# The RWKV recurrence in 45 named pieces: another order, 64x64 score products, and an inverse by two blocks of 8 and a corner

## The chip, the cores and the metric

The kernel runs on one core of one Trainium2 chip. The metric is device time in microseconds from launch to the last output. Before the change the median of three runs is 3890.82 us (3889.8 to 3914.53). TensorE is called PE below, VectorE DVE, ScalarE ACT, GpSimd POOL; SP is the engine that issues the DMAs.

## The reference, cut to what matters

Two blocks run one after the other on 512 tokens of width 1024. The first has a Fourier layer and an RWKV layer, each followed by a mixture of experts; the second has two attention layers with feed-forward parts. The change touches the recurrence of the RWKV layer alone. Per direction (forward and reversed) and per head (16 heads of 64) the reference scans the tokens one by one, first 256 context tokens, then the 512 tokens of x, with a 64x64 state:

```python
def step(s, inp):
    r_t, w_t, k_t, v_t, a_t, b_t = inp
    sa = jnp.einsum('bhvk,bhk->bhv', s, a_t)
    s = s * w_t[:, :, None, :] + sa[..., None] * b_t[:, :, None, :] + v_t[..., None] * k_t[:, :, None, :]
    return s, jnp.einsum('bhvk,bhk->bhv', s, r_t)
```

The outputs of the context tokens are not needed; only the state that they leave is.

## The kernel before, in words

`c_scan` (from L1357) does not go token by token but chunk by chunk: 64 tokens are one chunk, and a step of the loop takes one chunk of each of the two directions for all 16 heads. There are 12 steps: 4 of context, then 8 of x. Inside a chunk the recurrence is a triangular system of 64 unknowns per head. A step is done in three stages, which the loop of L1604 onwards overlaps: round `i` runs `products(i+2)` and `inverse(i+2)`, `merge(i+1)` and `advance(i)`; two rounds, -2 and -1, fill the pipeline.

- `products` (L1411): the scores of a chunk, 64x128 weights (`bk`) by 64 columns in context steps and 128 in x steps (`ar`), into `Aps` in PSUM (L1430); DVE multiplies them with a triangular mask into `GA` (L1434); PE turns `bk` (`bkp`, L1439) and ACT copies the result to `bkN` (L1441). This is done four times a step (two directions, two groups of four head pairs), each piece with two `Aps` tiles.
- `inverse` (L1447): the 16x16 diagonal blocks of the triangular matrices are brought onto lanes (ACT `Dg` L1453, DVE transpose `W` L1456, `A` L1458), and all of them are inverted by forward substitution: for the rows t = 1 to 15 one DVE product of t x t elements per lane (`pr`, L1464) and one DVE sum (L1465), each waiting for the one ahead.
- `merge` (L1468): two doublings, 16 to 32 to 64, by small products (`m` L1485, `tt` L1492, `m` L1506, `x` L1519; called m2, tt, m4 and x4 below) with DVE transposes (`T` L1479, `TT` L1480, `T` L1497) and ACT copies between them. After m4 the matrices in `GA` are overwritten by four DMAs (L1511) with what the state product needs; this is called the refill below.
- `advance` (L1526): the recurrence of the state: product `G` (L1542), copy `Gs`, product `U` with the inverse (L1551), copy `UV`, product `S` (L1568), then `sn` (DVE L1574), the decayed state `sd` (POOL L1562), and the new state `SV` (L1576), one half of the partitions by DVE and one by POOL. In x steps the output follows: `Yps` (L1584 and L1588) and its copy or sum into `Y` (L1597, L1599).

The order of the work is written as a string (L1603) of letters, one for a piece, in which G, U, S, Y stand for the pieces of `advance`, p, i and m or M for the next piece of the other stages:

```python
order = "M G p g p M pp M p mpp" + " U u pppp pp M pp m" + " p S pp i p M s m ii iii iii" + " Y i ii M i y ii m ii i"
```

This is not the order of the instructions on an engine. A planner takes the written order as a priority: it plays the program through with its own costs, and for each engine it takes, of the instructions that are ready by these costs, the one that was written first. What comes out is fixed; on the chip each engine then works its list strictly in turn. PSUM has eight banks: three for the scores (pool `pA`), two for the turns and the doublings (`pm`), three for G, U, S and the output (`pc`).

Of the kernel before, what the change touches and what calls it, by code (L numbers as in the profile page):

```python
# [11 lines left out]
F32 = mybir.dt.float32  # L12
# [24 lines left out]


# [1318 lines left out]
def c_scan(e, sp, PL, Y):  # L1357
# [4 lines left out]
    with ExitStack() as ctx:  # L1362
# [48 lines left out]
        def products(i):  # L1411


            st = sts[i]
            isc, chs = steps[i]
            na = 1 if isc else 2
            ga = st["GA"] = p3.tile([P, 2, ND, 2, 2, 64], F32, name="GA")
            bkN = st["bkN"] = p3.tile([P, 2, ND, P], F32, name="bkN")
# [4 lines left out]
            for d in range(2):  # L1423
                ar, bk = st["ar"][d], st["bk"][d]
                flat = lambda dt: bk[:, dt].rearrange("p a t -> p (a t)")
                for g in range(2):
                    pss = [pA.tile([P, 4, P], F32, name="Aps") for hh in range(2)]
                    for b in range(4):
                        for hh in range(2):
                            nc.tensor.matmul(pss[hh][:, b, :64 * na], flat(4 * g + b)[hv[hh]], ar[hv[hh], 4 * g + b, 0:na, :],  # L1430
                                             start=True, stop=True, tile_position=(64 * hh, 0))
                    yield
                    for hh in range(2):
                        tt_(ga[:, d, 4 * g:4 * g + 4, hh, 0:na, :].rearrange("p a r t -> p a (r t)"), pss[hh][:, :, :64 * na],  # L1434
                            bc(mgl[d][hh][:, :64 * na], 4), ALU.mult)
                    yield
                    ps = pm.tile([P, 4, P], F32, name="bkp", tag="mm")
                    for b in range(4):
                        nc.tensor.transpose(ps[:, b, :], flat(4 * g + b), e.ident)  # L1439
                    yield  # L1440
                    nc.scalar.copy(bkN[:, d, 4 * g:4 * g + 4, :], ps)  # L1441
                    yield

        def parts(st):
            return [q4(st["GA"], q)[:, :, :, q // 2, 0, :].rearrange("p c d t -> p (c d) t") for q in range(4)]

        def inverse(i):  # L1447

            st = sts[i]
            Ev = parts(st)  # L1450
            Dg = p1.tile([P, 16, 32], F32, name="Dg", tag="t3")
            for q in range(4):
                nc.scalar.copy(q4(Dg, q), Ev[q][:, :, bs(q % 2)])  # L1453
            yield
            W = p1.tile([P, 16, 32], F32, name="W", tag="t1")
            nc.vector.transpose(W, Dg.rearrange("p u (s t) -> p t s u", s=2))  # L1456
            A16 = p1.tile([P, 16, 16], F32, name="A16")
            nc.vector.scalar_tensor_tensor(A16, W[:, :, 0:16], h16[:, 0:1], W[:, :, 16:32], op0=ALU.mult, op1=ALU.add)  # L1458
            X = st["X"] = p1.tile([P, 16, 16], F32, name="X", bufs=2)
            nc.gpsimd.tensor_copy(X, e.tc_("eye16").rearrange("p (a b) -> p a b", a=16))  # L1460
            yield
            for t in range(1, 16):
                pr = p1.tile([P, 15, 15], F32, name="pr")
                tt_(pr[:, :t, :t], bc(A16[:, t, :t], t), X[:, :t, :t].rearrange("p i j -> p j i"), ALU.mult)  # L1464
                nc.vector.tensor_reduce(X[:, t, :t], pr[:, :t, :t], op=ALU.add, axis=AX.X)  # L1465
                yield

        def merge(i):  # L1468

            st = sts[i]  # L1470
            chs = steps[i][1]
            ga, X, Ev = st["GA"], st["X"], parts(st)
            Tx = p1.tile([P, 16, 2, 16], F32, name="Tx", tag="t2")
            for s in range(2):
                nc.scalar.activation(Tx[:, :, s, :], X, AF.Copy, scale=h16[:, s:s + 1])
            yield
            TT16 = p1.tile([P, 16, 32], F32, name="TT16")
            T16 = p1.tile([P, 16, 32], F32, name="T16")
            nc.vector.transpose(T16.rearrange("p u (s j) -> p j s u", s=2), Tx.rearrange("p t s j -> p j s t"))  # L1479
            nc.vector.transpose(TT16.rearrange("p u (s t) -> p t s u", s=2), Tx.rearrange("p t s j -> p t (s j)"))  # L1480
            yield
            ps = pm.tile([P, 16, 32], F32, name="m2", tag="mm")
            for u in range(16):
                for q in range(4):
                    nc.tensor.matmul(q4(ps, q)[:, u, :], Ev[q][:, u, bs(q % 2)], q4(T16, q)[:, u, :], start=True, stop=True, tile_position=pos(q, q))  # L1485
            yield
            nc.scalar.activation(M2[:, :, 0:16], ps[:, :, 0:16], AF.Copy, scale=h16[:, 1:2])
            yield
            ps = pm.tile([P, 16, 32], F32, name="tt2", tag="mm")
            for u in range(16):  # L1490
                for q in range(4):
                    nc.tensor.matmul(q4(ps, q)[:, u, :], q4(M2, q)[:, u, :], q4(TT16, q)[:, u, :], start=True, stop=True, tile_position=pos(q, q))  # L1492
            yield
            TT32 = p1.tile([P, 16, 32], F32, name="TT32")
            tt_(TT32, ps, TT16, ALU.add)
            T32 = p1.tile([P, 16, 32], F32, name="T32", tag="t2")
            nc.vector.transpose(T32, TT32)  # L1497
            TT64 = st["TT64"] = TT64s[i % 2]
            for h2 in (0, 2):
                nc.scalar.copy(q4(TT64, h2)[:, :, bs(0)], q4(TT32, h2))  # L1500
                nc.gpsimd.tensor_copy(q4(TT64, h2 + 1)[:, :, bs(1)], q4(TT32, h2 + 1))
            yield
            ps = pm.tile([P, 16, 32], F32, name="m4", tag="mm")
            for u in range(16):
                for h2 in (0, 2):
                    nc.tensor.matmul(q4(ps, h2 + 1)[:, u, :], Ev[h2][:, u, bs(1)], q4(T32, h2)[:, u, :], start=True, stop=True,  # L1506
                                     tile_position=pos(h2, h2 + 1))
            yield
# [3 lines left out]
            M4 = p1.tile([P, 16, 32], F32, name="M4", tag="t3")  # L1512
            for h2 in (0, 2):
                nc.scalar.copy(q4(M4, h2 + 1), q4(ps, h2 + 1))
            yield
            ps = pm.tile([P, 16, 32], F32, name="x4", tag="mm")
            for u in range(16):
                for h2 in (0, 2):
                    nc.tensor.matmul(q4(ps, h2)[:, u, :], q4(M4, h2 + 1)[:, u, :], q4(TT32, h2 + 1)[:, u, :], start=True, stop=True,  # L1519
                                     tile_position=pos(h2 + 1, h2))  # L1520
            yield
            for h2 in (0, 2):
                nc.scalar.copy(q4(TT64, h2)[:, :, bs(1)], q4(ps, h2))
            yield

        def advance(i):  # L1526

            isc, chs = steps[i]
            st = sts[i]
            ga, bkN, TT64, SV = (st[k] for k in ("GA", "bkN", "TT64", "SV"))  # L1530
            last = i == n - 1
            pl_ = [PL[d][:, chs[d], :] for d in range(2)]
            both = [(dt, hh) for dt in range(ND) for hh in range(2)]
            UV = [p3.tile([P, ND, 2, 64], F32, name="UV", bufs=2) for d in range(2)]
            for d in range(2):
                values(UV[d], chs[d])
            if not last:
                states(i + 1)
            ps = [pc.tile([P, ND, 64], F32, name="G", tag="c") for d in range(2)]
            for d in range(2):  # L1540
                for dt, hh in both:
                    nc.tensor.matmul(ps[d][hv[hh], dt, :], ga[:, d, dt, hh, 0, :], SV[d][:, dt, hh, :], start=True, stop=True, tile_position=(0, 64 * hh))  # L1542
            yield
            Gs = [p2.tile([P, ND, 64], F32, name="Gs") for d in range(2)]
            for d in range(2):
                nc.scalar.copy(Gs[d], ps[d])
# [803 lines left out]
```

## Time and profile before

| | |
|---|---|
| median of three runs | 3890.82 us |
| the profiled execution: its time | 3894.26 us |
| its span (first to last instruction) | 3892.5 us |
| PE busy | 3585.0 us, 92% of the span |
| DVE, ACT, POOL busy | 1762.6, 1115.3, 545.2 us |
| PE granted clock, mean | 0.93 of full speed |
| the recurrence | from 1300 to 1744 us of the span |

The page gives shares over the whole span; the change lies in the 444 us of the recurrence, so everything below is read from that stretch. A granted clock of 0.5 is 1.2 GHz, one of 1.0 is 2.4 GHz. A row of the timeline merges instructions of one line that follow each other; its second number is their time from the first start to the last end.

### The profile page before, as it was taken

How to read it: one execution, taken by the hardware profiler on the slowest of the kernel's cores; microseconds unless marked ns; L12 is line 12 of the kernel's file. 1: busy time of each engine (PE TensorE's matmuls, PEld its weight loads, DVE VectorE, ACT ScalarE, POOL GpSimd, SP SyncE). 2: the span in 40 equal slices, each digit the busy share in tenths (PEclk: the TensorE clock that was granted, in tenths of full speed). 3: DMA queues.
4: the chain of work that ended last, by engine and by line, in shares of the span. 5: the costliest groups of instructions: out<-in, count | busy, mean ns of one | idle time of the engine just before them, and what ended most of it. 6: DMA issues, size and time to landing. Idle time of an engine off the chain costs nothing. (4 is left out here: it accounts for less than half of the span.)

```text
span 3892.5 us, 66006 instructions
## 1 busy us (share of the span) xinstructions
PE 3585.0 (92%) x28088; PEld 2259.5 (58%) x28088; DVE 1762.6 (45%) x3424; ACT 1115.3 (29%) x1974; POOL 545.2 (14%) x429
## 2 busy tenths in 40 slices
PE   8889999978998686779999999999999989999999
PEld 4633333335777575668533324566788756567886
DVE  4512322246355566565221215865544458454443
ACT  3311111125366243332200002433322234342222
POOL 3100000002023122120100002220111222201111
PEclk8989999989998577788899999999999989999999
DMA  7489989934656644332899995111233321113332
GB/s 281 179 337 367 360 325 372 346 109 132 199 123 169 142 128 121 100 92 86 340 409 394 409 394 164 28 48 31 85 97 93 90 70 33 40 32 103 93 97 76
DMA packets 585853, 690.39 MB, mean 177 GB/s; under 512 B 178825, under 2 KB 454111, under 8 KB 585046
## 3 DMA queue, kind: packets, MB, share of 16 engines
q1 hardware_dynamic: 579344, 666.54, 50.6%
q10 hardware_dynamic: 3686, 11.09, 0.8%
q0 software_dynamic: 2528, 8.53, 0.6%
q8 instruction: 221, 3.62, 0.4%
q14 instruction: 74, 0.61, 0.0%
HBM read 646.24 MB, written 39.85 MB: 176 GB/s over the span
## 5 line engine op out<-in xcount | busy, mean ns | idle before, releaser
L894 ACT CAST whi<-wraw 128x1024 fp32r<-128x1024 f32 (+3 forms) x236 | 233.2, 989 | 707.2 <-issue 223.9
L641 PE MATMUL GU<-we,Xe 128*32 128x512 f32 x2048 | 304.4, 599 | 3.4 <-DVE hid L646 3.4
L895 DVE TENSOR_TENSOR wlo<-wraw,whi 128x1024 fp32r<-128x1024 f32 (+3 forms) x196 | 231.8, 1183 | 108.1 <-ACT whi L894 99.4
L666 PE MATMUL Y<-we,hidT 128*32 128x512 f32 x2048 | 261.3, 595 | 5.0 <-DVE Zc L698 3.5
L641 PE MATMUL GU<-we,Xq 128*32 128x512 f32 x2048 | 252.0, 611 | 0.0
L646 DVE TENSOR_TENSOR hid<-hid,GU 64x1536 f32<-64x1536 f32 (+1 forms) x32 | 47.7, 1491 | 359.4 <-ACT hid L645 359.4
L641 PE MATMUL GU<-we,Xc 128*32 128x512 f32 x1024 | 188.9, 596 | 0.0
L645 ACT ACTIVATE hid<-GU 64x1536 f32<-64x1536 f32 (+1 forms) x32 | 39.3, 1229 | 457.7 <-PE GU L641 457.7
L1884 POOL TENSOR_TENSOR u<-u 128x512 f32<-128x512 f32 x64 | 93.9, 1469 | 533.2 <-ACT uph L1883 533.2
L641 PEld LDWEIGHTS GU<-we,Xe 128*32 128x32 f32 x2048 | 78.8, 110 | 150.9 <-issue 145.2
L641 PEld LDWEIGHTS GU<-we,Xq 128*32 128x32 f32 x2048 | 67.7, 113 | 160.8 <-issue 157.9
L930 PE MATMUL pj<-hTh,whi 128*128 128x512 f32 (+1 forms) x352 | 154.5, 440 | 4.1 <-ACT hTh L1013 2.8
L666 PEld LDWEIGHTS Y<-we,hidT 128*32 128x32 f32 x2048 | 70.2, 110 | 148.1 <-issue 143.4
L932 PE MATMUL pj<-hTh,wlo 128*128 128x512 f32 (+1 forms) x352 | 148.7, 423 | 0.0
L931 PE MATMUL pj<-hTl,whi 128*128 128x512 f32 (+1 forms) x352 | 147.6, 419 | 0.0
L895 POOL TENSOR_TENSOR wlo<-wraw,whi 128x1024 fp32r<-128x1024 f32 x40 | 96.1, 2403 | 311.3 <-ACT whi L894 291.5
L930 PE MATMUL pj<-xh,whi 128*128 128x512 f32 (+1 forms) x320 | 118.2, 369 | 9.2 <-ACT whi L894 9.2
L1430 PE MATMUL Aps<-ar,bk 64*128 64x128 f32 (+1 forms) x768 | 98.3, 367 | 27.1 <-DVE GA L1434 25.1
L655 DVE COPY hidT<-htp 128x512 f32<-128x512 f32 (+1 forms) x48 | 27.6, 600 | 209.3 <-PE htp L654 121.4
L711 DVE SCALAR_TENSOR_TENSOR xres<-sps,mod,xres 128x512 f32<-128x512 f32 x128 | 89.0, 745 | 65.1 <-PE sps L710 64.5
L932 PE MATMUL pj<-xh,wlo 128*128 128x512 f32 (+1 forms) x320 | 115.4, 361 | 1.6 <-DVE wlo L895 1.6
L931 PE MATMUL pj<-xl,whi 128*128 128x512 f32 (+1 forms) x320 | 114.8, 359 | 0.0
(2151 smaller groups left out, 7929.4 us busy)
## 6 DMA issues: line engine op xcount, KB each, us to landing
we<-in_moe_wd_dram SPq DMA_DIRECT2D x128, 1024.0 KB
we<-in_moe_wg_dram SPq DMA_DIRECT2D x126, 1024.0 KB
we<-in_moe_wu_dram SPq DMA_DIRECT2D x126, 1024.0 KB
ada<-in_ada_w_dram SPq DMA_DIRECT2D x32, 1024.0 KB
wraw<-in_w_up_dram SPq DMA_DIRECT2D x64, 512.0 KB
wraw<-in_w_down_dram SPq DMA_DIRECT2D x64, 512.0 KB
wraw<-in_w_in_dram SPq DMA_DIRECT2D x42, 512.0 KB
adw<-in_ada_w_dram SPq DMA_DIRECT2D x32, 512.0 KB
```

The source lines that it names most:

```text
L641: nc.tensor.matmul(GU[j:j + 32, g, :], xs[g][:, kk, :], ws[m][:, k, h * 512:(h + 1) * 512], start=kk == 0, stop=kk == 7, tile_position=(0, j))
L645: nc.scalar.activation(hid[up], GU[lo], AF.Silu)
L646: nc.vector.tensor_tensor(hid[up], hid[up], GU[up], ALU.mult)
L666: nc.tensor.matmul(Y[j:j + 32, 0, :], hidT[:, g, k, 32 * kh:32 * kh + 32], w[:, kh, h * 512:(h + 1) * 512], start=kh + k == 0, stop=kh * k ...
L711: nc.vector.scalar_tensor_tensor(r_[:, c, :], ps, g2[:, c, s:s + 1], r_[:, c, :], op0=ALU.mult, op1=ALU.add)
L894: e.nc.scalar.copy(hi, src)
L895: (eng or e.nc.vector).tensor_tensor(lo, src, hi, ALU.subtract)
L930: nc.tensor.matmul(ps, a[0], b[0], start=start, stop=False)
L931: nc.tensor.matmul(ps, a[0], b[1], start=False, stop=False)
L932: nc.tensor.matmul(ps, a[1], b[0], start=False, stop=stop)
L1430: nc.tensor.matmul(pss[hh][:, b, :64 * na], flat(4 * g + b)[hv[hh]], ar[hv[hh], 4 * g + b, 0:na, :], start=True, stop=True, tile_position= ...
L1884: nc.gpsimd.tensor_tensor(u, u, u, ALU.mult)
```

## The change: what it does

`products`, `inverse`, `merge` and `advance` are cut into 45 named functions, and a round calls them in the order of the string `ORDER`: A and E are scores and mask of a group, B and C a turn and its copy, Dg, W, I0 to I4 and Tx the inverse, T16, m2, M2, tt, TT32, T32, Tc, Td, m4, R (the refill), M4, x4, X4 the doublings, Ga to Vb the recurrence for each direction (a and b) by itself, d its `sd` on POOL, Ya, Yc, qa, qb the output. Each piece names the step it belongs to (the offset 0, 1 or 2). The planner stays as it is.

Besides the order: a score product is cut into two of 64x64 weights, which go to the four quarters of the array; the inverse treats the two 8x8 blocks of each 16x16 block together for the rows 1 to 7 and then finds the corner below by two products of 8x8x8; both halves of the new state are added by DVE; PSUM is divided 4, 2, 2 instead of 3, 2, 3; some SBUF tiles that shared a place have their own.

```diff
+ORDER = """A1 A0 da B1 E1 B0 Ga Gb C1 ga gb T16 E0 Ua A3 E3 ua m2 db Sa M2 A2 Ub va C0 tt Va E2 TT32 ub Dg B2 T32 Sb vb m4 W I0 Ya I1
+           M4 I2 C2 Yc qa R B3 x4 Td Tc I3 qb X4 I4 C3 Vb Tx"""
...
-        pA = ctx.enter_context(tc.tile_pool(name="sA", bufs=3, space=PSUM, reuse_waits="tile"))
+        pA = ctx.enter_context(tc.tile_pool(name="sA", bufs=4, space=PSUM, reuse_waits="tile"))
         pm = ctx.enter_context(tc.tile_pool(name="sm", bufs=2, space=PSUM, reuse_waits="tile"))
-        pc = ctx.enter_context(tc.tile_pool(name="sc", bufs=3, space=PSUM, reuse_waits="tile"))
+        pc = ctx.enter_context(tc.tile_pool(name="sc", bufs=2, space=PSUM, reuse_waits="tile"))
...
-                            nc.tensor.matmul(pss[hh][:, b, :64 * na], flat(4 * g + b)[hv[hh]], ar[hv[hh], 4 * g + b, 0:na, :],
-                                             start=True, stop=True, tile_position=(64 * hh, 0))
...
+        def score(i, g):
+            st = sts[i]
+            d, g = g // 2, 4 * (g % 2)
+            na = 1 if steps[i][0] else 2
...
+            for b in range(4):
+                for j in range(2):
                     for hh in range(2):
+                        k = (hh + j) % 2
+                        nc.tensor.matmul(pss[hh][hv[k], b, :64 * na], st["bk"][d][hv[hh], g + b, k, :], st["ar"][d][hv[hh], g + b, 0:na, :],
+                                         start=True, stop=True, tile_position=(64 * hh, 64 * k))
...
-            for t in range(1, 16):
-                pr = p1.tile([P, 15, 15], F32, name="pr")
-                tt_(pr[:, :t, :t], bc(A16[:, t, :t], t), X[:, :t, :t].rearrange("p i j -> p j i"), ALU.mult)
-                nc.vector.tensor_reduce(X[:, t, :t], pr[:, :t, :t], op=ALU.add, axis=AX.X)
-                yield
...
+        def rows(i, ts):
             st = sts[i]
+            A, X = diag(st["A16"]), diag(st["Xf"])
+            for t in ts:
+                pr = p1.tile([P, 8, 8, 8], F32, name="pr")[:, 0:2, :t, :t]
+                tt_(pr, A[:, :, t, :t].unsqueeze(2).to_broadcast([P, 2, t, t]), X[:, :, :t, :t].rearrange("p b i j -> p b j i"), ALU.mult)
+                nc.vector.tensor_reduce(X[:, :, t, :t], pr, op=ALU.add, axis=AX.X)
+
+        def corner(i, second):
...
+            pr = p1.tile([P, 8, 8, 8], F32, name="pr")
+            tt_(pr, a.unsqueeze(2).to_broadcast([P, 8, 8, 8]), b.rearrange("p i j -> p j i").unsqueeze(1).to_broadcast([P, 8, 8, 8]), ALU.mult)
+            nc.vector.tensor_reduce(o, pr, op=ALU.add, axis=AX.X)
+
...
+        for k, ts in enumerate(((1, 2, 3), (4, 5), (6, 7))):
+            ops[f"I{k}"] = (2, lambda i, ts=ts: rows(i, ts))
+        for k in range(2):
+            ops[f"I{3 + k}"] = (2, lambda i, k=k: corner(i, k))
...
+        def refill(i):
             for d in range(2):
                 for hh in range(2):
-                    nc.sync.dma_start(ga[hv[hh], d, :, hh, 0, :], sp[f"ar{d}"][hv[hh], chs[d], :, 0, :])
...
+                    nc.sync.dma_start(sts[i]["GA"][hv[hh], d, :, hh, 0, :], sp[f"ar{d}"][hv[hh], steps[i][1][d], :, 0, :])
...
-                        (nc.gpsimd if hh else nc.vector).tensor_tensor(sts[i + 1]["SV"][d][hv[hh], :, hh, :], sn[hv[hh]], sd[d][hv[hh]], ALU.add)
...
+            elif k == "V":
+                sn, sd = st.pop(("sn", d)), st.pop(("sd", d))
+                for hh in range(2):
+                    tt_(sts[i + 1]["SV"][d][hv[hh], :, hh, :], sn[hv[hh]], sd[hv[hh]], ALU.add)
...
-        order = "M G p g p M pp M p mpp" + " U u pppp pp M pp m" + " p S pp i p M s m ii iii iii" + " Y i ii M i y ii m ii i"
...
+        order = ORDER.split()
+        assert sorted(order) == sorted(ops)
...
         for i in range(-2, n):
...
+            for k in order:
+                if k == "m4" and i + 3 < n:
                     load(i + 3)
-                if g is not None:
-                    next(g, None)
...
+                j, f = ops[k]
+                if 0 <= i + j < n:
+                    f(i + j)
```

## Rows read from the trace of the kernel before

**Rows 1.** The page's part 1: busy us, share of the span, instructions.
```profile
PE 3585.0 (92%) x28088; PEld 2259.5 (58%) x28088; DVE 1762.6 (45%) x3424; ACT 1115.3 (29%) x1974; POOL 545.2 (14%) x429
```

**Rows 2.** Windows of the recurrence: stretch, length, busy us per engine, clock, DMA.
```profile
1300.00:1350.00 50.00, 42.19 (x614) 39.02 (x616) 28.83 (x89) 14.22 (x25) 1.62 (x3) 0.53 0.51 115
1350.00:1407.00 57.00, 46.79 (x1293) 41.90 (x1294) 41.00 (x95) 26.82 (x48) 17.59 (x18) 0.80 0.56 144
1407.00:1481.00 74.00, 53.17 (x1417) 45.77 (x1416) 49.10 (x98) 27.62 (x49) 18.38 (x19) 0.68 0.47 123
1481.00:1677.00 196.00, 144.12 (x3851) 127.14 (x3854) 123.78 (x243) 70.34 (x122) 43.58 (x44) 0.79 0.40 104
1677.00:1730.00 53.00, 43.45 (x1440) 39.56 (x1430) 29.75 (x57) 19.22 (x34) 13.06 (x12) 0.79 0.21 46
...
1300.00:1744.00 444.00, 342.56 (x8840) 302.51 (x8840) 274.27 (x582) 162.54 (x284) 94.24 (x96) 0.75 0.43 109
```

**Rows 3.** Windows of one round, G to G; then of tile `pr` alone.
```profile
1555.40:1592.10 36.70, 25.53 (x786) 22.63 (x784) 24.59 (x48) 14.39 (x25) 8.79 (x9) 0.87 0.45 117
...
1555.40:1592.10 36.70, 0.00 (x0) 0.00 (x0) 11.46 (x30) 0.87 0.45 117
```

**Rows 4.** Timeline of PE and SP: start, us, engine, line, idle before.
```profile
1524.29 1.15 PE L1542 MATMUL G<-SV,GA 128*64 128x64 f32 x30
1526.26 1.15 PE L1551 MATMUL U<-Gs,TT 64*64 64x64 f32 x32
1527.82 1.16 PE L1430 MATMUL Aps<-ar,bk 64*128 64x128 f32 x16
1528.91 1.29 PE L1492 MATMUL tt<-TT,M 32*32 32x32 f32 x128
1535.28 2.08 PE L1584 MATMUL Yps<-GA,UV 128*64 128x64 f32 x64
1540.44 0.66 PE L1439 MATMUL bkp<-tab,bk 128*128 128x128 f32 x4
1541.03 1.38 PE L1430 MATMUL Aps<-ar,bk 64*128 64x128 f32 x18
1552.41 1.93 PE L1485 MATMUL m<-T,GA 32*32 32x32 f32 x128 [10.01 <-DVE T L1479]
...
1571.57 3.03 SPq L1511 DMA_DIRECT2D GA<-sp_ar  x4
1595.44 1.97 PE L1542 MATMUL G<-SV,GA 128*64 128x64 f32 x30
```

**Rows 5.** Timeline of DVE, ACT and POOL in the same round.
```profile
1529.01 1.29 DVE L1434 TENSOR_TENSOR GA<-Aps,k_tabc 128x512 f32<-128x512 f32 x2 [1.82 <-PE Aps L1430]
1529.79 2.52 ACT L1453 COPY Dg<-GA 32x512 f32<-32x512 f32 x4 [0.55 <-DVE GA L1434]
1532.34 1.08 DVE L1456 STREAM_TRANSPOSE W<-Dg 128x512 f32<-128x512 f32 x1 [1.35 <-ACT Dg L1453]
1537.77 0.67 DVE L1576 TENSOR_TENSOR SV<-sn,sd 64x512 f32<-64x512 f32 x1
1540.66 2.15 POOL L1562 TENSOR_TENSOR sd<-SV,PL 64x512 f32<-64x512 f32 x2
1541.98 0.89 DVE L1464 TENSOR_TENSOR pr<-A,X 128x25 f32<-128x25 f32 x1
1544.11 0.27 DVE L1464 TENSOR_TENSOR pr<-A,X 128x64 f32<-128x64 f32 x1
1549.16 0.54 DVE L1464 TENSOR_TENSOR pr<-A,X 128x225 f32<-128x225 f32 x1
1549.74 0.39 DVE L1465 TENSOR_REDUCE X<-pr 128x15 f32<-128x225 f32 x1
1550.22 0.91 ACT L1475 ACTIVATE Tx<-X,k_tabc 128x256 f32<-128x256 f32 x2 [7.89 <-DVE X L1465]
1551.16 1.10 DVE L1479 STREAM_TRANSPOSE T<-Tx 128x512 f32<-128x512 f32 x1 [1.03 <-ACT Tx L1475]
```

More of the change, by code (lines that the diff above doesn't have):

```diff
@@ new lines, in scored, with turn @@
+        def scored(i, g):
+            st = sts[i]
+            d, g = g // 2, 4 * (g % 2)
+            na = 1 if steps[i][0] else 2
+            for hh, ps in enumerate(st["ps"].pop((d, g))):
+                tt_(st["GA"][:, d, g:g + 4, hh, 0:na, :].rearrange("p a r t -> p a (r t)"), ps[:, :, :64 * na], bc(mgl[d][hh][:, :64 * na], 4), ALU.mult)
+        def turn(i, g):
+            st = sts[i]
+            d, g = g // 2, 4 * (g % 2)
+            ps = st["pB", d, g] = pm.tile([P, 4, P], F32, name="bkp", tag="mm")
+            for b in range(4):
+                nc.tensor.transpose(ps[:, b, :], st["bk"][d][:, g + b].rearrange("p a t -> p (a t)"), e.ident)
@@ L1449, in inverse, with turned, gather @@
+        def turned(i, g):
+            st = sts[i]
+            d, g = g // 2, 4 * (g % 2)
+            nc.scalar.copy(st["bkN"][:, d, g:g + 4, :], st.pop(("pB", d, g)))
+        for g in range(4):
+            for k, f in zip("AEBC", (score, scored, turn, turned)):
+                ops[f"{k}{g}"] = (2, lambda i, f=f, g=g: f(i, g))
+        def gather(i):
             st = sts[i]
             Ev = parts(st)
-            Dg = p1.tile([P, 16, 32], F32, name="Dg", tag="t3")
+            Dg = st["Dg"] = p1.tile([P, 16, 32], F32, name="Dg")
@@ new lines, in m2, with m2out, t32, t32t @@
+        def m2(i):
+            Ev = parts(sts[i])
+            blocks(i, "m2", range(4), lambda q: Ev[q][:, :, bs(q % 2)], lambda q: q4(sts[i]["T16"], q))
+        def m2out(i):
+            nc.scalar.activation(M2[:, :, 0:16], sts[i].pop("m2")[:, :, 0:16], AF.Copy, scale=h16[:, 1:2])
+        def t32(i):
+            st = sts[i]
+            st["TT32"] = p1.tile([P, 16, 32], F32, name="TT32")
+            tt_(st["TT32"], st.pop("tt2"), st["TT16"], ALU.add)
+        def t32t(i):
+            sts[i]["T32"] = p1.tile([P, 16, 32], F32, name="T32")
+            nc.vector.transpose(sts[i]["T32"], sts[i]["TT32"])
@@ L1524, in merge, with x4, x4out @@
-            yield
-        def advance(i):
+        def x4(i):
+            blocks(i, "x4", (1, 3), lambda q: q4(sts[i]["M4"], q), lambda q: q4(sts[i]["TT32"], q), -1)
+        def x4out(i):
+            ps = sts[i].pop("x4")
+            for h2 in (0, 2):
+                nc.scalar.copy(q4(TT64s[i % 2], h2)[:, :, bs(1)], q4(ps, h2))
+        ops["Tx"] = (2, pairs)
+        ops["tt"] = (1, lambda i: blocks(i, "tt2", range(4), lambda q: q4(M2, q), lambda q: q4(sts[i]["TT16"], q)))
+        for k, f in (("T16", both16), ("m2", m2), ("M2", m2out), ("TT32", t32), ("T32", t32t), ("Tc", lambda i: t32c(i, 0)),
+                     ("Td", lambda i: t32c(i, 1)), ("m4", m4), ("R", refill), ("M4", m4out), ("x4", x4), ("X4", x4out)):
+            ops[k] = (1, f)
@@ L1528, in advance, with chain @@
+        def chain(i, d, k):
             isc, chs = steps[i]
             st = sts[i]
-            ga, bkN, TT64, SV = (st[k] for k in ("GA", "bkN", "TT64", "SV"))
+            SV, UV = st["SV"][d], st["UV"][d]
             last = i == n - 1
-            pl_ = [PL[d][:, chs[d], :] for d in range(2)]
-            both = [(dt, hh) for dt in range(ND) for hh in range(2)]
-            UV = [p3.tile([P, ND, 2, 64], F32, name="UV", bufs=2) for d in range(2)]
-            for d in range(2):
-                values(UV[d], chs[d])
@@ L1538, in advance, with enter_, y128 @@
+        for k in "GgUuSvVd":
+            for d in range(2):
+                ops[k + "ab"[d]] = (0, lambda i, d=d, k=k: chain(i, d, k))
+        def enter_(i):
+            sts[i]["UV"] = [p3.tile([P, ND, 2, 64], F32, name="UV", bufs=2) for d in range(2)]
+            for d in range(2):
+                values(sts[i]["UV"][d], steps[i][1][d])
+            if i < n - 1:
                 states(i + 1)
-            ps = [pc.tile([P, ND, 64], F32, name="G", tag="c") for d in range(2)]
+        def y128(i):
+            st = sts[i]
+            st["Y"] = [pc.tile([P, ND, 64], F32, name="Yps", tag="c") for d in range(2)]
@@ L1549, in advance, with y64 @@
+        def y64(i):
+            st = sts[i]
             for d in range(2):
                 for dt, hh in both:
[L1551 to L1557 removed]
@@ L1619, in c_scan @@
[L1619 to L1627 removed]
+                begin(i + 2)
+            for k in order:
+                if k == "m4" and i + 3 < n:
+                    load(i + 3)
+                j, f = ops[k]
+                if 0 <= i + j < n:
+                    f(i + j)
```

257 lines of the change are left out of this document (109 added, 148 removed).

## The prediction

> **What bounds the kernel now.** The page's shares come first, and they mislead: PE is busy 92% of the span [rows 1], but the change touches only the recurrence. The windows view cuts that out: in its 444 us PE is busy 342.6 us, at a mean granted clock of 0.75, DVE 274 us [rows 2]. No engine is full, so a chain must set the time. A chunk of x takes 36.7 us from one G to the next; DVE works 24.6 us of it, 11.5 us on tile `pr`, the substitution [rows 3]. The timeline shows the chain. PE ends its last scores at 1542.41 and stands idle 10.01 us until the transpose T, then starts m2, and only behind m2 come most of the state's products G [rows 4]. On DVE in that gap the last rows of the substitution run (1549.16, 1549.74), then Tx on ACT, then T [rows 5]. So the substitution on DVE and the products on PE run mostly one after the other. After the gap PE is at the lower clock, 1.2 GHz: 30 G instructions take 1.97 us at 1595.44 against 1.15 us at 1524.29 [rows 4]. A second loss: beside POOL's `sd` a product of 25 elements takes 0.89 us on DVE, one of 64 elements without it 0.27 us [rows 5].
>
> **The change, part by part.** The sum is made against the profiled execution, 3894.26 us (span 3892.5 and 1.8 around it); the median is 3.4 us below it.
>
> Substitution. It had 15 products and 15 sums; now it has 7 of each on two blocks, with 2, 8, ... 98 elements (280 in all), and two corners of 512 elements. Between 64 and 225 elements a product grows from 0.27 to 0.54 us, 1.68 ns an element on a base of 0.16 [rows 5]. Seven products are then 7 x 0.16 + 280 x 0.00168 = 1.6 us; the sums, at 0.39/0.54 of a product, 1.15; 14 gaps of 0.04 (1549.70 to 1549.74) 0.6: together 3.3. A corner is 0.16 + 512 x 0.00168 = 1.02 for the product, 0.74 for the sum and 0.08 of gaps; two are 3.7. In all 7.0 us against 11.5. No row shows a corner. Its product lies between 0.67 us (SV, 512 elements from two SBUF operands) and 1.23 (0.54 x 512/225); I take the line through the nearest rows. This leaves 6 to 8 us for the whole.
>
> The second half of SV goes from POOL to DVE: 2 x 0.67 = 1.34 us. DVE then has 24.6 - 11.5 + 7.0 + 1.3 = 21.4 us a round. `sd` stays on POOL but is written behind A0 and behind m2, beside masks and transposes rather than beside the substitution; whether that holds is a rival below.
>
> Scores. 16 instructions with 128 columns of weights become 32 with 64, on four quarters instead of two halves. Before, a group takes 1.16 us [rows 4]. After, no row shows four quarters at work. If all four run at once, U's row (32 instructions with 64 columns of weights on two quarters, 1.15 us) halves to 0.58; if only two do, and the 128 moving columns double it, 2.3. I take 1.16, since the multiplications and weights are the same: no gain, with -2.3 to +4.6 us of PE a round as ends. The other way to see it is by instruction count: 128 products of 32x32 take 1.29 us, 10 ns each [rows 4], so 64 more instructions a round need not cost by their number. The Trainium skill, "TensorEngine Tiling (Array Packing)", section Instruction Overhead, says that each product has an overhead of some 60 cycles and warns against cutting a dimension that is already small; as an estimate from that page, 64 x 25 ns over 12 rounds is 19 us and the time 3782. The trace disagrees with that rule.
>
> Order. The three loops of an x round, at the full clock:
> PE: scores 4 x 1.16, turns 4 x 0.66, G and U 2 x 1.15 each, S 2.1, m2 and tt 1.29 each, m4 and x4 no more than that each, output 2 x 2.08: 23.3 us.
> DVE: 21.4 us, as above.
> The ring through the engines: A2 1.16, E2 1.29 (and 0.9 because Va is ahead of it on DVE), Dg 2.52, W 1.08 and A 0.5, substitution 7.0, Tx 0.91 (Vb beside it runs 0.4 longer), E1 1.29, T 1.10, m2 1.29, Sa 1.04, then A2 again; eight handoffs of 0.15 (T to m2: 1552.26 to 1552.41): 21.7 us.
> What changes is that G, U and two score groups now stand ahead of m2, so PE works while DVE does Vb, E1 and T. I walked one round piece by piece with these durations: PE never waits longer than it takes to hand over. In it, PSUM is no bound: A3 waits for E1's two banks and m2 for C1, both done a microsecond or more ahead. U of direction b waits for ua with only two `pc` banks, but m2, Sa and A2 lie between. DVE behind T has va waiting for Sa; E2, TT32 and the substitution are queued behind it, and PE needs TT32 only for m4. The refill R comes after m4; before the next G are Ya, Yc, B3, x4, A1, A0, B1 and B0, 9.7 us, against 20.5 us now (1571.57 to 1592.11). Its issue takes 3.03 us on SP, where UV's and SV's loads, which also wait for the end of Y, are queued behind it; landing should be covered; if not, G waits, a rival. PE needs 23.3; I add 1.7 for collisions of three nearly equal loops: 25 us an x round.
>
> Rounds 0 and 1 have no output (4.2 us less on PE) and half-wide masks: ring-bound, 21 each. Rounds 2 and 3: no output, 23 each. The lead of 50 us loses 4.5 us of substitution once and some 3 us because the doublings of step 0 no longer share DVE with the rows of step 1: 42. Round 8 adds its output on DVE (0.7), so 126 for rounds 4 to 8; rounds 9 and 10 take 25 + 21, for round 10 prepares nothing. The last 14 us stay. The sum by the stretches of [rows 2]: 42 + 42 + 46 + 126 + 46 + 14 = 316 us in place of 444. 128 us go: 3894.3 - 128 = 3766, and 3763 against the median. Behind the recurrence the work starts earlier by as much; its weights are loaded from where SBUF comes free, so I cost that at nothing.
>
> **Rivals.**
> POOL still beside DVE (17%). The planner issues `sd` and the copies Td when they are ready by its own costs; if they fall on substitution or SV again, five products lose 0.7 each and an SV about 1: 4.5 us a round. DVE becomes the bound at 26, a round 29.5: 10 rounds lose 45, 3808. For it: it is so today. Against: `sd` needs only the old state, and comes early.
> The planner puts PE behind the inverse again (13%): the written order is only a priority, and today m2 stands ahead of G though G is written first. Then the 10 us idle shrinks only by 4.5 us, 12 rounds and the lead give 57: 3834. Against: SV no longer waits for POOL.
> The refill is late (5%). If landing needs the 20.5 us that it has today, G waits 10.8 us, a round is 35.8: 12 us gained over the x rounds and little before: 3875, within 1%.
> Slower (4%). If PE's idle is cut into many short waits and the clock stays at 1.2 GHz, all products take 1.97/1.15 = 1.71 times as long: 40 us an x round, 33 without output. The stretches become 50 + 66 + 66 + 200 + 73 + 22 = 477, and waits of 1.7 us in 12 rounds make it 497: 3944. It decides from a mean clock near 0.55 in rounds 4 to 8, against 0.79 now [rows 2]. Against: PE would be the fullest engine, and in the dense stretch from 1522 to 1542 it ran at full clock.
>
> **The numbers.** The forecast has 61%, its own range is 3730 to 3795 (rounds of 22.5 us to the high end of the scores). The range for 8 in 10 reaches over POOL and most of the planner's case: 3730 to 3832. About 1% (39 us) is what a measurement of this kernel can tell from no change. Faster by more: forecast, POOL and planner, 0.91; within: the late refill, 0.05; slower: 0.04.
>
> **What would show it.** G to G in x rounds of 24 to 26 us; no idle of 10 us ahead of m2; a clock above 0.9 in the x rounds; the tile `pr` at 7 us a round or less; a score group of 0.6 to 1.2 us at the full clock; `sd` not beside `pr`; no wait of G for a DMA. The prediction is wrong if PE waits for T, or for `Aps` to be emptied, more than 3 us a round, or if rounds stay over 31 us.

## The result, and the profile after

The changed kernel takes 3839.94 us (median of 4 runs) against 3895.66 us of the kernel before in the same measurement: a ratio of 0.986, with a 95% interval of 0.981 to 0.990. The interval leaves out 1, so the gain is clear of the noise. The profiled execution takes 3837.1 us, 57 less than the one of before. The forecast was 3763, a gain of 128. The sign was right, the size less than half.

The page's part 1 (busy us, share, instructions) hardly moves against [rows 1]; PE has 768 more products in its list.

```profile
PE 3550.5 (93%) x28856; PEld 2219.0 (58%) x28856; DVE 1735.9 (45%) x3302; ACT 1113.7 (29%) x1974; POOL 512.3 (13%) x407
```

Windows of the recurrence (columns as in [rows 2]), cut where G starts: the lead, rounds 0 and 1, 2 and 3, 4 to 8, 9 and 10, the last, and then the whole.

```profile
1298.00:1331.20 33.20, 22.42 (x759) 18.64 (x757) 23.31 (x62) 14.34 (x26) 1.62 (x3) 0.76 0.66 148
1331.20:1393.50 62.30, 49.33 (x1441) 42.08 (x1437) 44.10 (x81) 27.75 (x50) 13.22 (x15) 0.77 0.54 135
1393.50:1458.10 64.60, 45.98 (x1444) 38.89 (x1441) 42.79 (x77) 26.20 (x46) 11.54 (x14) 0.84 0.52 140
1458.10:1621.40 163.30, 132.35 (x4244) 114.01 (x4241) 107.97 (x193) 69.70 (x123) 28.45 (x34) 0.91 0.49 127
1621.40:1671.90 50.50, 41.80 (x1468) 37.70 (x1465) 26.94 (x48) 18.26 (x32) 6.58 (x8) 0.88 0.22 47
...
1298.00:1686.00 388.00, 305.96 (x9603) 261.48 (x9601) 248.56 (x462) 163.15 (x288) 61.42 (x74) 0.86 0.48 122
```

The recurrence has lost 56 us (444 to 388), nearly the whole gain. Rounds 4 to 8 take 163 us, 32.7 each; 25 were forecast. PE is busy 81% there at a clock of 0.91, DVE 66%: still a chain. The timeline of PE at the start of a round shows it (idle before and its releaser in brackets).

```profile
1515.93 0.66 PE L1459 MATMUL bkp<-tab,bk 128*128 128x128 f32 x4 [0.68 <-ACT TT L1589]
1516.52 1.98 PE L1444 MATMUL Aps<-ar,bk 64*64 64x128 f32 x64
1521.08 1.72 PE L1444 MATMUL Aps<-ar,bk 64*64 64x128 f32 x16 [2.58 <-DVE GA L1452]
1522.73 0.47 PE L1608 MATMUL G<-SV,GA 128*64 128x64 f32 x2
1523.13 1.13 PE L1444 MATMUL Aps<-ar,bk 64*64 64x128 f32 x16
1524.19 0.53 PE L1542 MATMUL m<-T,GA 32*32 32x32 f32 x20
1524.65 1.97 PE L1608 MATMUL G<-SV,GA 128*64 128x64 f32 x30
```

Two score groups run (A1, A0), then the third (A3) waits for the masks, which must empty its PSUM banks. G stands behind it and comes in pieces of 2 and 30, with scores and m2 between. After the wait 30 G take 1.97 us, as at the half clock of [rows 4]; the granted clock from 1524.7 to 1526.6 is 0.50. The timelines of DVE, POOL and SP say why the masks are late:

```profile
1509.25 0.99 DVE L1498 TENSOR_TENSOR pr<-A,X 128x8 f32<-128x8 f32 x1
1510.47 0.90 DVE L1498 TENSOR_TENSOR pr<-A,X 128x18 f32<-128x18 f32 x1
1515.62 1.09 DVE L1512 TENSOR_TENSOR pr<-X,Yc 128x512 f32<-128x512 f32 x1
1516.74 0.69 DVE L1513 TENSOR_REDUCE X<-pr 128x64 f32<-128x512 f32 x1
1518.48 1.13 DVE L1534 STREAM_TRANSPOSE T<-Tx 128x512 f32<-128x512 f32 x1 [1.06 <-ACT Tx L1527]
1519.49 1.01 DVE L1535 STREAM_TRANSPOSE TT<-Tx 128x512 f32<-128x512 f32 x1
1520.35 2.47 DVE L1452 TENSOR_TENSOR GA<-Aps,k_tabc 128x512 f32<-128x512 f32 x4
...
1509.17 2.15 POOL L1626 TENSOR_TENSOR sd<-SV,PL 64x512 f32<-64x512 f32 x2 [2.49 <-DVE SV L1637]
...
1506.59 2.85 SPq L1575 DMA_DIRECT2D GA<-sp_ar  x4
```

The masks (2.47) stand behind the substitution and behind both transposes, though the first mask was written ahead of them. POOL's `sd` falls beside the substitution again, and products of 8 and 18 elements take 0.99 and 0.90. The refill was issued at 1506.59, 16 us ahead of G, and no G waits for a DMA. Over the recurrence PE's waits (us in total, times, longest) begin so:

```profile
PE Aps L1444 <- DVE GA L1452: 40.7, 15, 7.3
PE m L1542 <- issue: 6.1, 9, 1.5
```

### The profile page after: what moved, and what is told of

Same layout as the page of the kernel before. It is cut to its first block, busy times and chain, and to the rows that moved or that the text cites. A ratio compares the mean times of both kernels' runs of the same rounds, so it can differ in the third digit from the quotient of the medians.

```text
span 3835.3 us, 67418 instructions
## 1 busy us (share of the span) xinstructions
PE 3550.5 (93%) x28856; PEld 2219.0 (58%) x28856; DVE 1735.9 (45%) x3302; ACT 1113.7 (29%) x1974; POOL 512.3 (13%) x407
## 5 line engine op out<-in xcount | busy, mean ns | idle before, releaser
L1444 PE MATMUL Aps<-ar,bk 64*64 64x128 f32 (+1 forms) x1536 | 67.9, 307 | 41.8 <-DVE GA L1452 40.7
```

What stands on the lines that cost most here:

```text
L1444: nc.tensor.matmul(pss[hh][hv[k], b, :64 * na], st["bk"][d][hv[hh], g + b, k, :], st["ar"][d][hv[hh], g + b, 0:na, :], start=True, stop=Tr ...
```

## The experiments

Theory A: the planner's order is what is lost. It had G wait for the refill by its own prices and put A3 and m2 ahead of it. Theory B: PE's own work sets the round. Theory C: `sd` beside the substitution does. Later came D: PE waits for its own instructions, which come late behind data, and E, against it: these gaps have no link to the data. Last F against R: whether the supply of instructions (F) or the ring through DVE (R) sets the floor of a round.

The names of the runs say which order they have: those that begin with "written" keep the pieces in the written order on PE, DVE, ACT and POOL, like all_as_written; those that begin with "after" leave them to the planner, like the changed kernel. "x round" is a fifth of the time between the first U of round 4 and that of round 9; the waits are PE's, for masks and "issue" (it waited for nothing that the view of waits shows), summed over 1410 to 1620 us of the span. Both come from the one profiled execution of each run, so small differences in them carry no interval; the ratios do. In the kernel before, the main wait of this stretch is another: 35.8 us for the transpose T.

| run | ratio to before, 95% | x round us | masks, issue us |
|---|---|---|---|
| before | 1 | 39.1 | 7.8, 3.4 |
| changed kernel | 0.986 (0.981 to 0.990) | 32.7 | 30.7, 8.4 |
| loads_after_refill | 0.980 (0.977 to 0.984) | 32.4 | 0.3, 31.5 |
| pe_as_written | 0.982 (0.979 to 0.985) | 31.0 | 0, 36.8 |
| all_as_written | 0.977 (0.974 to 0.981) | 30.4 | 0, 40.3 |
| no_corner | 0.980 (0.976 to 0.983) | 30.6 | 3.3, 15.8 |
| written_values_2kb | 0.974 (0.970 to 0.978) | 28.4 | 0, 31.6 |
| after_values_2kb | 0.973 (0.969 to 0.977) | 30.1 | 0, 25.3 |
| written_wide_scores | 0.976 (0.972 to 0.979) | 28.6 | 0, 34.7 |
| after_old_inverse | 0.984 (0.980 to 0.989) | 33.4 | 33.5, 7.7 |
| written_no_loads | 0.971 (0.968 to 0.973) | 25.8 | 0, 25.7 |
| written_old_inverse | 0.981 (0.978 to 0.983) | 30.8 | 0, 30.3 |
| written_less_traffic | 0.974 (0.971 to 0.977) | 27.9 | 0, 31.8 |
| after_less_traffic | 0.975 (0.973 to 0.978) | 28.1 | 0, 22.6 |
| written_no_loads_wide | 0.968 (0.967 to 0.970) | 24.2 | 0, 16.5 |
| written_no_loads_no_corner | 0.967 (0.965 to 0.969) | 25.5 | 0, 24.9 |
| after_order_alone | 0.991 (0.988 to 0.994) | 34.8 | 27.2, 1.3 |

**Order: loads_after_refill, pe_as_written, all_as_written, no_corner.**

```diff
-                if k == "m4" and i + 3 < n:          # loads_after_refill
+                if k == "B3" and i + 3 < n:
...
-        for i in range(-2, n):
+        with tc.manual_schedule(engines={mybir.EngineType.PE}):       # pe_as_written; all_as_written: also DVE, Activation, Pool
+            for i in range(-2, n):
...
-        order = ORDER.split()                        # no_corner
+        order = [k for k in ORDER.split() if k not in ("I3", "I4")]
```

> One edit: the four loads of step i+3 are issued behind the refill of GA instead of ahead of m4. Theory A (the planner prices the refill as landing behind these loads, so it puts a third score group and pieces of m2 ahead of G; on the chip that third group waits for masks that stand behind the substitution, and G, U, S and the new state wait with it): G stands right behind x4, the wait of TensorE for masks ahead of G (2.6 to 7.3 us a round) is gone, an x round takes 26 to 28 us instead of 32 to 33, the kernel 3790 to 3805. Theory B (order is not the matter, the 26 us of TensorE's own work at the clock it gets, and its small issue gaps, set the round): x rounds 31 to 33, 3830 to 3845. Theory C (the two state multiplies on GpSimd that fall beside the substitution rows are the loss): untouched by this edit, 3830 to 3845. If the loads now land late, the first scores wait for a DMA and up to 3 us a round come back.

> One edit: TensorE issues the pieces of the recurrence in the written order (all other engines as the planner likes). Theory A: G stands behind the first two score groups and the turns and ahead of the third score group and of m2; x rounds 26 to 28 us, 3790 to 3805. Theory B: x rounds 31 to 33, 3830 to 3845. Theory C: 3830 to 3845.

> One edit: TensorE, VectorE, ScalarE and GpSimd all issue the pieces of the recurrence in the written order. This also takes the state multiplies of GpSimd away from the substitution rows and puts the first mask ahead of T16. Theory A alone: as with TensorE alone, 3790 to 3805. A and C together (the substitution stretch falls from 9.3 to about 7.5 us): 1 to 2 us a round less, 3775 to 3795. C alone: 3815 to 3825. Theory B: 3830 to 3845.

> The two corner products and sums of the inverse are left out (3.6 us of VectorE in each round), so the inverse lacks its lower left quarter of every 16x16 block. Theory A: the ring substitution, T16, masks, third score group, G, U, S, new state, masks, substitution runs through VectorE's corner, so each round shortens by about 3.6 us: 3800 to 3810. Theory B: TensorE's own work sets the round, VectorE only idles longer: 3830 to 3840.

What the one moved load does is seen in PE's list as the planner left it, from x4 to S, shortened (xN counts calls; the profile has two products for a call, but one for a turn). First the changed kernel, then loads_after_refill:

```
MATMUL x 32x32 x32 | bkp x8 | Aps x40 | G x1 | Aps x8 | m x10 | G x15 | m x19 | G x1 | U x16 | m x12 | G x15 | m x23 | S
MATMUL x 32x32 x32 | G x17 | U x16 | G x15 | bkp x8 | m x13 | Aps x48 | m x51 | S
```

G came in four pieces because the refill is four DMAs, and in the planner's account they land behind the 2 MB of loads issued ahead of them. With the loads behind the refill, G follows x4 at once. So the first half of A is shown: the order came from the planner's price for the refill. The second half fell: the mask wait went, as A expected, but "issue" waits took its place: PE's waits of all kinds in the same 210 us are 47.9 us in the changed kernel and 46.7, 48.9 and 45.1 in loads_after_refill, pe_as_written and all_as_written. The x round won 0.3, 1.7 and 2.3 us where 5 to 7 had been expected. B falls too, in part: all_as_written is faster than the changed kernel (0.977 against 0.986; the intervals just part). By the x round, PE waits 6.2 us in both; what all_as_written won is PE's busy time, 26.5 us to 24.2. Most of that is G, which no longer runs at half clock behind the mask wait. Over the five x rounds (busy us, mean ns), first the changed kernel, then all_as_written:

```profile
L1608 PE MATMUL G<-SV,GA 128*64 128x64 f32 x321 | 19.9, 272 | 0.0
```

```profile
L1608 PE MATMUL G<-SV,GA 128*64 128x64 f32 x321 | 10.9, 224 | 0.2 <-issue 0.2
```

In all_as_written `sd` stands beside transposes, and the same DVE products are fast:

```profile
1533.90 0.16 DVE L1498 TENSOR_TENSOR pr<-A,X 128x2 f32<-128x2 f32 x1
...
1534.29 0.17 DVE L1498 TENSOR_TENSOR pr<-A,X 128x8 f32<-128x8 f32 x1
...
1534.69 0.18 DVE L1498 TENSOR_TENSOR pr<-A,X 128x18 f32<-128x18 f32 x1
...
1540.26 0.69 DVE L1513 TENSOR_REDUCE X<-pr 128x64 f32<-128x512 f32 x1
```

So the collision of C is real (0.99 and 0.90 became 0.17 and 0.18), though what it alone is worth in time was not separated from the rest of the order. no_corner won 2.1 of the 3.6 us left out: between A and B. It is no clean test of the ring, for without the corners the planner also moved a piece of m2 ahead of the scores, and the mask wait nearly went (3.3 us).

**What "issue" is: written_values_2kb, after_values_2kb.** The gaps of all_as_written lie 128 products, or a multiple, apart (a few records are missing). The expectations put issue waits of 53 us and rounds of 29.7 us down for all_as_written; as this document sums them they are 56.3 and 30.4.

```diff
-                nc.sync.dma_start(t_[hv[1 - hh], :, hh, :], v[:, hh])
+                nc.sync.dma_start(t_[hv[1 - hh], hh], v[:, hh])     # SV and UV: [P, 2, ND, 64] for [P, ND, 2, 64]
```

> On the version with all four engines in the written order: the tiles SV and UV are laid out with each half contiguous, so that the value loads (1 MB a round) go in pieces of 2 KB instead of 256 B; nothing else. Seen so far: with the order mended, TensorE's waits with no visible cause (issue) grew from 17 to 53 us over the recurrence, and they lie 128 products (or a multiple) apart; 128 products and their 128 weight loads are 256 instructions, the size of one packet of the instruction queue (16 KB). Theory D (TensorE waits for its instruction blocks, which come late behind the data packets): half of the small packets gone, issue waits fall from 53 to 20 to 35 us, x rounds from 29.7 to 27.5 to 28.5, the kernel 3788 to 3802. Theory E (these gaps have nothing to do with the data traffic): 3805 to 3815, issue waits 45 to 60 us.

> The same layout of SV and UV on the changed kernel as it is, in the planner's order. Theory D with A (there the waits for masks hide the late blocks: issue waits are only 17 us): a gain of at most 10 us, 3830 to 3845. If the gain is as large as on the version in written order (10 to 20 us or more), the two limits don't hide each other. Theory E: no gain, 3838 to 3848.

On the written order it won 0.003 of the ratio (12 us, the intervals overlap): the x round is 2 us shorter, but the issue waits of the whole recurrence fell only from 56.3 to 50.7 us where D expected 20 to 35. D's number missed. On the changed kernel the gain, 0.013 (some 50 us), was far more than either theory expected, and not by D: cheaper value loads ahead of the refill changed the planner's list. G now follows A1, A0 and the turns in one piece, and of the waits (as above) the one for masks is nearly gone:

```profile
PE m L1542 <- issue: 16.5, 12, 2.9
PE m L1542 <- DVE T L1534: 10.6, 5, 3.7
...
PE Aps L1444 <- DVE GA L1452: 2.8, 5, 0.8
```

An edit of a layout is an edit of the order here. Nothing of the computation is left out in this kernel, and it beats the changed kernel and the one before (0.973 against 0.986 and 1, intervals apart); from written_values_2kb (0.974) it can't be told.

**Is it the traffic: written_no_loads, written_less_traffic, after_less_traffic.**

```diff
+            if i > 4:                                # written_no_loads; rc, UV, SV in the same way
+                sts[i]["ar"], sts[i]["bk"] = sts[4]["ar"], sts[4]["bk"]
+                return
...
-                    nc.sync.dma_start(rc[:, d], sp[f"ar{d}"][:, chs[d], :, 1, :])      # less_traffic
+                nc.scalar.copy(sts[i]["rc"][:, d], sts[i]["ar"][d][:, :, 1, :])        # piece Rc, behind Dg
```

> On the version in written order, the bulk loads of steps 5 and later (bk, ar, rc and the values of UV and SV, 3.7 of 4.2 MB a round) are left out: those steps compute on the data of step 4 and on old values; every instruction of the compute engines stays. Theory D (issue waits are instruction blocks late behind data packets): issue waits of TensorE fall from 53 to at most 20 us, the rounds from number 4 on from 29.7 to 24.5 to 26 us, the kernel 3770 to 3788. Theory E (gaps at block borders without any link to the data traffic, or rounds set by something else): issue waits 45 to 60 us, 3802 to 3815.

> Written order, values in 2 KB pieces, wide scores (half an instruction block less a round), and rc copied on ScalarE from the ar tile instead of loaded (2048 of the 4600 remaining small packets of a round; 1.3 us of ScalarE behind the gather). Theory D: issue waits 20 to 35 us, x rounds 27 to 28 us, 3782 to 3797. Theory E: 3798 to 3812.

> The same three edits on the changed kernel in the planner's order (which with the cheaper value loads has G ahead of the third score group, as written). Theory D: 3780 to 3797. Theory E: as with the 2 KB values alone, 3797 to 3808.

Without the loads the x round falls from 30.4 to 25.8 us, with every compute instruction still there. One stretch of 30 us each (columns of [rows 2]) and its instruction queue (packets, MB, share), first of all_as_written, then of written_no_loads:

```profile
1470.00:1500.00 30.00, 23.77 (x827) 21.32 (x824) 20.44 (x38) 14.19 (x26) 5.17 (x7) 0.90 0.53 144
...
q8 instruction: 7, 0.11, 1.5%
```

```profile
1470.00:1500.00 30.00, 26.39 (x983) 23.80 (x984) 24.38 (x43) 17.24 (x31) 5.76 (x7) 1.00 0.10 22
...
q8 instruction: 8, 0.13, 1.9%
```

983 products and 984 weight loads are 1967 instructions; in 8 packets of 16 KB that is some 250 a packet. And a stretch of PE of written_no_loads shows the gaps:

```profile
1480.02 0.82 PE L1550 MATMUL m<-T,GA 32*32 32x32 f32 x73 [0.95 <-issue]
1480.77 1.15 PE L1637 MATMUL S<-UV,bkN 128*64 128x64 f32 x32
1481.85 0.88 PE L1452 MATMUL Aps<-ar,bk 64*64 64x128 f32 x23
1483.48 0.54 PE L1452 MATMUL Aps<-ar,bk 64*64 64x128 f32 x9 [0.76 <-issue]
1483.76 1.10 PE L1623 MATMUL U<-Gs,TT 64*64 64x64 f32 x32
1484.79 0.94 PE L1550 MATMUL tt<-TT,M 32*32 32x32 f32 x87
1487.23 0.56 PE L1550 MATMUL tt<-TT,M 32*32 32x32 f32 x41 [1.51 <-issue]
```

73 + 32 + 23 is 128, 9 + 32 + 87 is 128: 256 instructions with their weight loads, one packet. The blocks begin 3.46 and 3.75 us apart though, of the bulk data, nothing but the refill moves. D expected at most 20 us of issue waits in the recurrence and was too bold: 37.9 are left. In the 210 us of the table they fell from 40.3 to 25.7, for 6619 products instead of 5780. The time came out as D said (0.971 is 27 us below all_as_written), and E falls.

What the waits are, the traces can settle, for they keep every packet of the instruction queue. The DMA view counts a packet by its start; cut to 0.1 us, its share (of 16 engines) gives the length as well. Windows 1481.1:1481.2 and 1484.6:1484.7 of written_no_loads, then 1458.6:1458.7 of all_as_written:

```profile
q8 instruction: 1, 0.02, 59.9%
```

```profile
q8 instruction: 1, 0.02, 84.2%
```

```profile
q8 instruction: 1, 0.02, 64.1%
```

These packets take 0.96, 1.35 and 1.03 us. The first starts at 1481.15, 1.13 us behind the first product of a block (1480.02), lands at 1482.11, and the next block begins 1.37 us later, at 1483.48: that is the whole 3.46. The second makes the 3.75 in the same way (1.16, 1.35, 1.25). In the 210 us, every one of the 28 issue waits of all_as_written and of the 27 of written_no_loads ends 1.2 to 1.7 us after such a packet has landed. So it is shown that these waits are waits for instructions. The data come in at the packet's start. In all_as_written, behind a block that began with a wait, the next packet starts 1.06 to 1.60 us after the block's first product where no data packet started in between (11 times), but 3.0 to 3.8 us after it where data ran at 300 GB/s or more (4 times, beside the loads of `ar` and `bk`). Those four are followed by waits of 4.22, 2.80, 1.99 and 4.62 us. Beside less data it took 1.06 to 2.65 us. In written_no_loads 26 of 27 start within 1.65 us; the other, at 3.79, has no data beside it, so data are not all that can hold a packet back. The packet itself takes as long with the loads as without (1.1 us, median).

Of the 4.6 us a round that went with the loads, 3.1 are waits (6.2 to 3.1 a round) and 1.5 PE's busy time (24.2 to 22.7), with the granted clock up from 0.90 to 0.97 over these rounds.

The less_traffic runs join three edits: 2 KB values, wide scores (below) and rc copied instead of loaded. The x rounds are 27.9 and 28.1 us, but neither time can be told from that with 2 KB values alone: written_less_traffic (3797.2 us) lies between D's range and E's, after_less_traffic (3802.8) in E's. What its x rounds won over after_values_2kb was lost ahead of them: the first U of round 4 starts at 1456.79 against 1449.38.

**Scores and inverse: written_wide_scores, after_old_inverse, written_old_inverse, after_order_alone.**

```diff
-                        nc.tensor.matmul(pss[hh][hv[k], b, :64 * na], st["bk"][d][hv[hh], g + b, k, :], ...   # 16 a group
+                    nc.tensor.matmul(pss[hh][:, b, :64 * na], st["bk"][d][hv[hh], g + b].rearrange("p a t -> p (a t)"), ...   # wide: 8 a group
...
+                tt_(pr[:, :t, :t], bc(A[:, t, :t], t), X[:, :t, :t].rearrange("p i j -> p j i"), ALU.mult)    # old inverse: t = 1..15
```

> On the version in written order: the scores go back to 64x128 products (64 fewer products and 64 fewer weight loads a round in the profile's count, half an instruction block). Forecast's pricing of the scores (quarters at 0.95 to 1.0 us a group against 1.16): 0.7 us a round lost, 3812 to 3822. Theory D (fewer instructions count): what the products lose comes back in issue waits, 3800 to 3812.

> The changed kernel with the inverse as before (15 rows on the whole 16x16 block). The inverse takes 11.5 instead of 7 us of VectorE a round. If the ring through VectorE sets the round in the changed kernel (leaving out 3.6 us of it gave 25 us in all, about 0.6 of what was left out): 0.6 to 1 times 4.5 us in 10 to 12 rounds, 27 to 54 us slower than the changed kernel, 3870 to 3897. If TensorE sets it: 3840 to 3855.

> On the version in written order, the inverse goes back to 15 rows on the whole 16x16 block (11.5 instead of 7 us of VectorE a round). With the changed kernel as it is, this cost nothing. If the planner's order was what hid the inverse's gain: 27 to 45 us slower than the written order with the new inverse, 3835 to 3855. If TensorE (instruction blocks) sets the round here too: 3805 to 3822.

> The changed kernel with both of its arithmetic parts undone: scores as 64x128 products and the inverse as 15 rows; what is left is the step in 45 pieces and the PSUM split. If the pieces alone earned the 57 us (the old inverse cost the changed kernel nothing, wide scores cost the written order nothing): 3835 to 3855. If the parts have a share that shows only when both are gone: 3860 to 3890.

The quarters earn nothing: with wide scores the time can't be told from that of all_as_written (0.976 and 0.977). Its x round is 1.8 us shorter, but its round 4 starts 8 us later (1460.35 against 1452.37). The old inverse costs the changed kernel nothing that the ratio shows, and the written order 0.003 (13 us, the intervals overlap); had the ring through DVE set the round, it would have been 27 us or more in both. The windows of the tile `pr` over five x rounds (DVE is the third number pair) show why, for the changed kernel, after_old_inverse, all_as_written and written_old_inverse in turn:

```profile
1458.10:1621.40 163.30, 0.00 (x0) 0.00 (x0) 39.81 (x90) 0.91 0.49 127
```

```profile
1460.40:1627.20 166.80, 0.00 (x0) 0.00 (x0) 48.13 (x150) 0.90 0.44 117
```

```profile
1452.40:1604.30 151.90, 0.00 (x0) 0.00 (x0) 32.15 (x90) 0.90 0.56 145
```

```profile
1444.90:1598.80 153.90, 0.00 (x0) 0.00 (x0) 40.62 (x150) 0.89 0.51 141
```

That is 9.6 us a round for the old inverse against 8.0 in the planner's order, and 8.1 against 6.4 in the written one: a gain of 1.7, not 4.5, in both. In after_old_inverse, moreover, the planner put two masks between the transposes (T16 at 1553.94, masks at 1554.92, TT16 at 1556.08), so undoing the inverse also undid a part of the bad order. With both parts undone (after_order_alone) the ratio is 0.991: the pieces, the PSUM split and both halves of SV on DVE alone earn 0.009, some 34 of the 57 us, and the two parts together the rest, if the medians are taken at their word (the intervals overlap).

**The floor: written_no_loads_wide, written_no_loads_no_corner** (both edits as above, put together).

> The version in written order without the bulk loads of steps 5 and later (left out as before), with the scores as 64x128 products: 64 fewer products and 64 fewer weight loads of about 852 each a round. Seen: without that traffic a round takes 25.3 us, and in its dense stretch TensorE's blocks of 128 products begin 3.3 to 3.75 us apart, each after a short issue wait. Theory F (the supply of instruction blocks sets the floor of a round): half a block less, 1.7 us a round in some 10 rounds, 3762 to 3772. Theory R (the ring through VectorE sets the floor): 3778 to 3790.

> The same version without bulk loads, with the two corner products and sums of the inverse left out as well (3.6 us of VectorE a round). Theory R (ring through VectorE): 2 to 3.6 us a round, 3748 to 3765. Theory F: 3774 to 3786.

Fewer instructions shorten the x round from 25.8 to 24.2 us, by 1.6 where F expected 1.7; the shorter ring shortens it by 0.3 where R expected 2 to 3.6. The 1.6 us went from PE's waits (3.1 to 1.7 us a round), not from its busy time (22.7 and 22.5). For the x rounds F stands, as far as one profiled execution of each tells. The total says less: 9 and 14 us, the first within the intervals, for the short ring wins ahead of the x rounds: its U of round 4 starts at 1441.97 against 1451.84, that of round 9 at 1569.36 against 1580.75. There the ring counts, as R says.

## Why the prediction was wrong

The step that failed is "G, U and two score groups now stand ahead of m2, so PE works while DVE does Vb, E1 and T. I walked one round piece by piece with these durations: PE never waits longer than it takes to hand over." The walk took the written order for the order on the engine. In the planner's list A3 and a piece of m2 stood ahead of most of G, and the rival that said so ("the planner puts PE behind the inverse again", 13%, 3834 us) came within 6 us of the time, by another wait than it named: PE waited 6.0 us for T in the whole recurrence and 40.7 for `Aps` to be emptied. So that number is luck. The prediction had named the wait for `Aps` as one that would prove it wrong (more than 3 us a round; 40.7 us over 12 rounds came). The sign of this was in the trace of before: G written first, standing in pieces. The argument "SV no longer waits for POOL" looked at the wrong operand; in the changed kernel the refill's price was what held G back. The rival "POOL still beside DVE" came true as well, but small: 1.5 us of `pr` a round (8.0 against 6.4) where five products were to lose 3.5.

A second term was missing from the walk: the supply of PE's instructions. With the order mended it takes the place of the mask waits. "64 more instructions a round need not cost by their number" was wrong for the written order: there they cost 1.6 to 1.8 us an x round (25.8 to 24.2 and 30.4 to 28.6), which over 12 rounds is about the 19 us that the prediction worked out and set aside, by another mechanism. In the totals that cost is not clear of noise. Products at 10 ns each show what PE can do with instructions that it has, not how fast they come.

Mis-sized was the inverse. The new one was priced well: in the written order the substitution runs from 1533.90 to 1540.95, 7.05 us against 7.0; corners take 1.02 and 1.10 (forecast 1.02) and 0.69 (0.74). But the 11.5 us that it replaces held collisions: with `sd` elsewhere the old inverse takes 8.1 (written_old_inverse). The change did not remove the collisions either (8.0 against 6.4). And 11.5 is busy time alone, while the 7.0 hold 0.8 of gaps. A saving measured beside a collision is not a saving of the operation.

Right were the sums of work. In written_no_loads PE is busy 22.7 us an x round (forecast 23.3), DVE 20.9 (21.4), and the clock is 0.97 over these rounds. That the round takes 25.8 us (25) is half luck: the 1.7 us added to PE's work were for collisions of the loops, and what stands there is 3.0 us of issue waits. Where two groups of scores took 1.98 us, a group cost 0.99, below the 1.16 taken. In the changed kernel the refill never made G wait.

By the ratios, times 3894: 56 us came with the change, the written order gives 32 more, leaving out the loads 27 more, wide scores 9 more: 124 of the 128 (each ratio is uncertain by 0.002 to 0.005, and the last step is within that). So nearly all of the forecast gain is reached only by a kernel without the planner's list, without the bulk loads and with one part of the change, the score quarters, undone.

## What to carry to other kernels

Where a planner makes the order, walk its list, not the written one: look for an operand that it believes late (pieces of one operation, one for each DMA, are the sign), and move the transfers that stand ahead of it. Before pricing a denser schedule on TensorE, count its instructions per us: when the waits that hid them go, "issue" waits at even distances in instructions show that the supply is next; whether each ends just behind a packet of the instruction queue decides it. A part is worth what undoing it costs in the version where nothing else hides it.

## What the hardware showed

PE's gaps without a visible cause lay 128 products and their 128 weight loads apart, the content of one 16 KB packet of the instruction queue, and each ended 1.2 to 1.7 us after such a packet had landed (55 of 55 in the 210 us of all_as_written and written_no_loads). In a dense stretch the blocks began 3.46 and 3.75 us apart with 22 GB/s of data moving; beside 300 GB/s or more a packet started up to 3.8 us behind its block instead of 1.06 to 1.60, and gaps of up to 4.6 us followed. The Trainium skill, "Runtime: NRT & Kernel Launch", section Instruction fetch mechanics, gives the same blocks (16 KiB, 256 instructions) and says that the cost of crossing a boundary is mostly hidden. The trace agrees on the block; on the cost it differs: 40 of 210 us in all_as_written (in the kernel before, where other waits cover it, 3.4). A group of 32 score products with 64x64 weights on four quarters of the array took 0.99 us, one of 16 with 64x128 took 1.16 [rows 4]; by the prediction's estimate two quarters at a time would have taken 2.3, so more than two ran at once. And a product of 8 elements on DVE took 0.99 us beside POOL's `sd` and 0.17 without it.
